# Four gate tiles move from single columns to column pairs of the seven-product form, and GpSimd takes part of the attention stage's vector work

## The chip, the cores and the metric

The kernel runs on one NeuronCore of a Trainium2 chip. A core has a matrix engine (TensorE, PE in the profile), a vector engine (VectorE, DVE), a scalar engine (ScalarE, ACT), GpSimd (POOL) and SyncE (SP), which issues the DMAs. The engines run their own instruction queues in order and meet at semaphores. The metric is the device time of one execution in microseconds (us); lower is better.

## The reference

One decoder block on a sequence of 1024 tokens of width 1024, all in float32. What matters here:

```
proj = rms_norm(x, ln1_g) @ w_in + b_in      # rq rk rv rg | aq ak av | gate_a gate_b
branch_a = (silu(rg) * head_group_norm(retention(rotary(rq), rotary(rk), rv))) @ w_ret_out
branch_b = sliding_window_sink_attention(rotary(aq), rotary(ak), av, sinks) @ w_attn_out
merged   = sigmoid(gate_a) * branch_a + sigmoid(gate_b) * branch_b
x = x + merged @ w_out
x = x + (silu(h2 @ w_ffn_gate) * (h2 @ w_ffn_up)) @ w_ffn_down    # h2 = rms_norm(x, ln2_g)
out = rms_norm(x, lnf_g)
```

`gate_a` and `gate_b` are 1024 columns each of the one projection: eight tiles of 128 columns each, called gate tiles 0 to 7 (first branch) and 8 to 15 (second). The attention has 16 query heads of 64, two key and value heads, blocks of 128 queries that look at 256 keys, and one sink per head.

## The kernel before

**Numbers.** A float32 operand is split into a high half in the fast matmul format (ScalarE, `copy`) and a low half, the rest (a subtraction), and a product is made of three matmuls: high by high, high by low, low by high. Every weight slab so costs one ScalarE cast and one subtraction (`split`, L129 to L137; for the query weights L401 and L402).

**Dense tiles.** `dense_g` makes one tile of 128 output columns for 1024 tokens: two halves of 512 tokens, 8 k-steps, 3 matmuls each, 48 matmuls of 128x512. Its weights (`slab`) pass through a ring of two buffers for high and low halves, so a new slab's halves are made when the tile two places earlier has done its last matmul.

**Column pairs.** After the attention the kernel computes wider pairs of tiles (256 columns, all 1024 tokens) with a seven-product scheme in the manner of Strassen: seven products of 12 matmuls, 84 in all, in place of 96. `cols` lists the pairs in order, `wseq` the order of their products, `wprep_to` makes the weight combinations (four GpSimd subtractions a pair, L555, and a split for each product, L130 and L133), `wproduct` multiplies, `wresult` evicts. Before, ten pairs are in `cols`: eight of the retention projections and two of the gates (tiles 2, 3 and 4, 5).

**The attention stage.** It has 32 units: four quads of four heads by eight blocks of queries. A unit u runs `u_scores` (eight matmuls of 256 columns into PSUM; for each of four heads a VectorE mask-and-minimum, L463, and a ScalarE exponential with its sum, L466; one reciprocal, L469; the four heads are scaled by it, L472 on ScalarE and L474 on VectorE, two each), `u_transpose` (eight transposes L484, then cast L487 and subtraction L488), and `u_values` (four matmuls L497 and L498, four small copies and sums L501 to L504, a split L506 and L507). GpSimd only puts the sink's column into the score tile `sc` (L451). Around the units stands fill, matmuls that wait for nothing of the units: `quad_q(g)` makes the queries of a quad (96 matmuls, then the rotation: eight VectorE and two ScalarE instructions a half, L419 to L428, into one buffer `stg`, and a round trip through DRAM), and `gate(n)` makes a dense gate tile, evicted with tanh (L513). `Fill` hands fill out in steps of three matmuls; the loop at the end of the stage gives each unit its share of `left` and lets `fl.until` force a quad's queries before its first unit. What stands on each engine's queue, and in which order, is chosen by the scheduler of the tile framework from the program order, priorities (`AHEAD`) and its own estimate; a queue then runs in exactly that order.

Fill before: queries of quads 1 to 3 and twelve gate tiles (6 to 15, 0, 1); of them the last three tiles are left for after the loop.

## Time and profile before

| what | value |
|---|---|
| time, median of 3 runs | 1584.97 us (1582.56 to 1584.98) |
| span of the profiled execution | 1583.3 us |
| PE, DVE, ACT, POOL busy, whole span | 1570.7, 990.2, 720.7, 354.9 us |
| loop over the attention units, first to last reciprocal | 101.9 to 323.6 us |
| seven-product stage of the pairs | about 435 to 626 us |
| granted TensorE clock | 0.999 |

The profiled execution's span is 1.7 us under the median of the runs. A row of a group of instructions reads: source line, engine, operation, output and inputs by the program's names, shapes, count | busy time, mean nanoseconds of one | idle time of the engine just before them and what ended it. A row of time reads: start, duration, engine, line, operation. Line numbers are those of the kernel before; the changed kernel's are one higher after the rotation's first new line.

### The profile page before, as it was taken

To read this page: it belongs to the slowest core of one execution; us is meant where nothing else is said; L and a number is where in the kernel's file an instruction comes from. 1 tells how busy PE (TensorE), PEld (TensorE's weight loads), DVE (VectorE), ACT (ScalarE), POOL (GpSimd) and SP (SyncE) were. 2 spreads that over 40 slices of the span, in tenths; PEclk is the share of its full clock that TensorE was granted. 3 is DMA by queue.
4 is the path that set the end of the run, shared out by engine and by line. 5 is a ranking of instruction groups with operands and counts; after the bars stand their busy time and mean duration, and the time that the engine had idled before them with its cause. 6 is when DMAs were issued, how large, how long until landed. Compare 5 with 4: busy or idle time off the path is not lost.

```text
span 1583.3 us, 20873 instructions
## 1 busy us (share of the span) xinstructions
PE 1570.7 (99%) x7483; PEld 1307.1 (83%) x7483; DVE 990.2 (63%) x1776; ACT 720.7 (46%) x1446; POOL 354.9 (22%) x303
## 2 busy tenths in 40 slices
PE   9999999999999999999999999999999999999998
PEld 8887888888888888888888888888888888888886
DVE  6469978777657663878544369444444444678656
ACT  5258877844233333544221256333333333344445
POOL 2000000000055441000000013555555555100001
PEclk9999999999999999999999999999999999999999
DMA  6564655440364455654545102333333333762333
GB/s 204 157 176 124 205 193 150 143 140 34 126 225 150 134 166 184 229 189 156 177 149 199 54 0 74 106 104 106 112 105 100 101 110 109 285 250 84 98 103 124
DMA packets 148886, 223.13 MB, mean 141 GB/s; under 512 B 9195, under 2 KB 81709, under 8 KB 147246
## 3 DMA queue, kind: packets, MB, share of 16 engines
q1 hardware_dynamic: 148780, 221.79, 43.3%
q8 instruction: 59, 0.97, 0.3%
q14 instruction: 45, 0.37, 0.1%
q10 hardware_dynamic: 2, 0.00, 0.0%
HBM read 149.67 MB, written 67.37 MB: 137 GB/s over the span
## 4 chain that ended last, share of the span: by engine, by line
PE 90%; ACT 6%; DVE 3%; issue 1%; POOL 0%; POOLq 0%; ACTq 0%; DVEq 0%
PE fA L1337 15%; PE fB L1337 8%; PE dA L1618 7%; PE wA L841 7%; PE dxP L1618 6%; PE fC L1337 4%; PE wB L841 3%; PE va L686 3%; ACT sc L466 2%; PE acc_g L157 2%; PE vP L686 2%; PE acc_g L158 2%; PE acc_g L159 2%; PE wo L1277 2%; PE wo L1276 2%; PE acc_ba L159 2%
## 5 line engine op out<-in xcount | busy, mean ns | idle before, releaser
L1618 PE MATMUL dA<-dwP,daP 128*128 128x512 f32 x528 | 120.6, 389 | 0.0
L1618 PEld LDWEIGHTS dA<-dwP,daP 128*128 128x128 f32 x528 | 99.0, 188 | 20.7 <-DVE dwP L133 0.2
L1618 PE MATMUL dxP<-dwP,daP 128*128 128x512 f32 x396 | 90.2, 389 | 0.0
L1618 PEld LDWEIGHTS dxP<-dwP,daP 128*128 128x128 f32 x396 | 74.3, 188 | 15.4
L157 PE MATMUL acc_g<-h,wh_g 128*128 128x512 f32 x192 | 75.5, 393 | 0.1
L158 PE MATMUL acc_g<-h,wh_g 128*128 128x512 f32 x192 | 75.2, 392 | 0.0
L159 PE MATMUL acc_g<-h,wl_g 128*128 128x512 f32 x192 | 75.1, 393 | 0.0
L466 ACT ACTIVATE sc<-sc,nm 128x257 f32<-128x257 f32 (+1 forms) x128 | 62.5, 492 | 27.1 <-DVE nm L463 26.7
L451 POOL COPY sc<-nsink 128x4 f32<-128x4 f32 x32 | 13.1, 412 | 274.4 <-PE pT L484 157.1
L1406 POOL TENSOR_TENSOR xf<-xf 128x512 f32<-128x512 f32 x40 | 61.2, 1531 | 30.4 <-issue 28.9
L1348 POOL TENSOR_TENSOR xf<-xf 128x512 f32<-128x512 f32 x33 | 49.4, 1496 | 54.3 <-ACT t_1P L130 22.4
L463 DVE CUSTOM_DVE_ANT_0 sc<-s,amask,nsink 128x256 f32<-128x256 f32 (+1 forms) x128 | 54.1, 461 | 9.8 <-PE s L460 9.5
L1358 ACT COPY xf<-fA 128x512 f32<-128x512 f32 x44 | 25.7, 586 | 74.4 <-PE fA L1337 74.4
L133 DVE TENSOR_TENSOR dwP<-wd,dwP 128x512 fp32r<-128x512 f32 x77 | 52.8, 685 | 6.0 <-ACT dwP L130 6.0
L130 ACT CAST dwP<-wd 128x512 fp32r<-128x512 f32 x77 | 47.4, 616 | 9.4 <-PE dA L1618 7.1
L157 PE MATMUL acc_bb<-ay,wh_bb 128*128 128x512 f32 x128 | 51.2, 400 | 0.0
L1523 POOL TENSOR_TENSOR rs_f<-tot,mhalf 128x1 f32<-128x1 f32 x8 | 4.8, 606 | 205.4 <-DVE tot L1520 205.4
L158 PE MATMUL acc_bb<-ay,wh_bb 128*128 128x512 f32 x128 | 50.3, 393 | 0.0
L159 PE MATMUL aq<-h,wl_aq 128*128 128x512 f32 x128 | 50.2, 392 | 0.0
L157 PE MATMUL aq<-h,wh_aq 128*128 128x512 f32 x128 | 50.1, 392 | 0.0
L158 PE MATMUL aq<-h,wh_aq 128*128 128x512 f32 x128 | 50.1, 391 | 0.0
L159 PE MATMUL acc_bb<-ay,wl_bb 128*128 128x512 f32 x128 | 50.1, 391 | 0.0
(794 smaller groups left out, 4356.9 us busy)
## 6 DMA issues: line engine op xcount, KB each, us to landing
act_d<-xf SPq DMA_DIRECT2D x77, 256.0 KB, 2.1
daP<-act_d SPq DMA_DIRECT2D x21, 512.0 KB
q_d<-stg SPq DMA_DIRECT2D x8, 1024.0 KB
q<-q_d SPq DMA_DIRECT2D x32, 256.0 KB, 6.5
ay_d<-q SPq DMA_DIRECT2D x8, 1024.0 KB
ay<-ay_d SPq DMA_DIRECT2D x4, 2048.0 KB, 14.2
wr_daP<-act_d SPq DMA_DIRECT2D x14, 512.0 KB, 3.7
wr_g<-in_w_in SPq DMA_DIRECT2D x12, 512.0 KB, 5.9
```

The source lines that it names most:

```text
L133: return nc.vector.tensor_tensor(out=lo, in0=raw, in1=f32(hi), op=ALU.subtract)
L157: nc.tensor.matmul(pt, hi[:, k, :], xh, start=(k == 0), stop=False)
L158: nc.tensor.matmul(pt, hi[:, k, :], xl, start=False, stop=False)
L159: nc.tensor.matmul(pt, lo[:, k, :], xh, start=False, stop=(k == 7))
L463: nc.vector.tensor_tensor_reduce(out=sc[:, j, 0:nk], in0=pt[:, jj * 256:jj * 256 + nk], in1=mk, scale=1.0, scalar=nsink[:, 4 * g + j:4 * g ...
L466: nc.scalar.activation(sc[:, j, 0:nk + 1], sc[:, j, 0:nk + 1], AF.Exp, scale=-1.0, bias=nm[:, j:j + 1], accum_out=den[:, j:j + 1])
L686: nc.tensor.matmul(vbanks[pr][tt], x_[:, c], w[:, u, :], start=(fresh and k + z == 0), stop=(k == 3 and z == 2), skip_group_check=not fresh)
L841: nc.tensor.matmul(pt, o[:, w, k, :], v, start=(first and k + z == 0), stop=(k == 3 and z == 2), skip_group_check=not first)
L1337: nc.tensor.matmul(pt, o[:, w, k, :], v, start=(first and k + z == 0), stop=(k == 3 and z == 2), skip_group_check=not first)
L1348: nc.gpsimd.tensor_tensor(out=dst[q], in0=dst[q], in1=sg[q], op=ALU.mult)
L1406: nc.gpsimd.tensor_tensor(out=o, in0=a, in1=b, op=op)
L1618: nc.tensor.matmul(banks[tt], a[:, u, c], w[:, v, :], start=(fresh and f + z == 0), stop=(f == NP - 1 and z == 2), skip_group_check=not fresh)
```

## The change

Tiles 0, 1, 6 and 7 leave the attention stage's fill and become two more column pairs in the seven-product stage, so that all eight gate tiles of the first branch are pairs (twelve pairs in `cols`). The fill keeps quads 1 to 3 and gate tiles 8 to 15, one gate behind each quad, the rest at the end; the count of steps follows, and three tiles are again left for after the loop. In the attention stage GpSimd makes the low halves of the gate weights and of the query weights of quads 1 to 3, three of the eight rotation steps of these quads (`s3 = b*cos`, `s0 = a*sin`, their sum), and the scaling of the fourth head of each unit, which ScalarE made.

```diff
-    def split(raw, hi, lo, hold=False):
+    def split(raw, hi, lo, hold=False, eng=None):
...
-            return nc.vector.tensor_tensor(out=lo, in0=raw, in1=f32(hi), op=ALU.subtract)
+            return (eng or nc.vector).tensor_tensor(out=lo, in0=raw, in1=f32(hi), op=ALU.subtract)
...
-                    nc.vector.tensor_tensor(out=lo, in0=rv_[:, :, z], in1=f32(hi), op=ALU.subtract)
+                    (nc.gpsimd if g else nc.vector).tensor_tensor(out=lo, in0=rv_[:, :, z], in1=f32(hi), op=ALU.subtract)
...
+                second = nc.gpsimd if g else nc.vector
+                second.tensor_tensor(out=s3, in0=b, in1=cos, op=ALU.mult)
+                nc.vector.tensor_tensor(out=s1, in0=b, in1=sin, op=ALU.mult)
                 nc.vector.tensor_tensor(out=s2, in0=a, in1=cos, op=ALU.mult)
-                nc.vector.tensor_tensor(out=s1, in0=b, in1=sin, op=ALU.mult)
+                second.tensor_tensor(out=s0, in0=a, in1=sin, op=ALU.mult)
                 nc.vector.tensor_tensor(out=s2, in0=s2, in1=s1, op=ALU.subtract)
-                nc.vector.tensor_tensor(out=s0, in0=a, in1=sin, op=ALU.mult)
-                nc.vector.tensor_tensor(out=s3, in0=b, in1=cos, op=ALU.mult)
-                nc.vector.tensor_tensor(out=s3, in0=s3, in1=s0, op=ALU.add)
+                second.tensor_tensor(out=s3, in0=s3, in1=s0, op=ALU.add)
...
-                if j % 2:
+                if j == 1:
                     nc.scalar.activation(sc[:, j, 0:nk], sc[:, j, 0:nk], AF.Copy, scale=rd[:, j:j + 1])
                 else:
-                    nc.vector.tensor_scalar(out=sc[:, j, 0:nk], in0=sc[:, j, 0:nk], scalar1=rd[:, j:j + 1],
-                                            scalar2=None, op0=ALU.mult)
+                    (nc.gpsimd if j == 3 else nc.vector).tensor_scalar(out=sc[:, j, 0:nk], in0=sc[:, j, 0:nk],
+                                                                       scalar1=rd[:, j:j + 1], scalar2=None, op0=ALU.mult)
...
-            return dense_g(w_in, C_GA + n * P, H, evac, f"g{n}")
+            return dense_g(w_in, C_GA + n * P, H, evac, f"g{n}", nc.gpsimd)
...
-        order = list(range(6, 16))
+        order = list(range(8, 16))
         gens = []
-        for g in range(4):
-            gens += [quad_q(g + 1)] if g < 3 else []
-            gens += [gate(n) for n in (order[2 * g:2 * g + 2] if g < 3 else order[6:] + [0, 1])]
+        for g in range(3):
+            gens += [quad_q(g + 1), gate(order[g])]
+        gens += [gate(n) for n in order[3:]]
...
-        left = 32 * 8 - 8 - 20
+        left = 32 * 3 + 16 * len(order) - 40 - 20
...
-                fl.until(3 * (i // NB - 1) + 1)
+                fl.until(2 * (i // NB - 1) + 1)
...
-    cols += [C_GA + 256, C_GA + 512]
+    cols += [C_GA + 256 * i for i in range(4)]
```

Three places of the order, before and after. In the names, `sc13` is the score tile of quad 1, block 3 (the number behind the underscore is the program's), `rd` its reciprocals, `wl` a low half, `g11` gate tile 11, `stg21` the rotation's buffer of quad 2, second half.

GpSimd's queue in the middle of quad 1's units, before:

```order
L451 COPY sc13_1825<-nsink_85 128x4
L451 COPY sc14_1908<-nsink_85 128x4
L451 COPY sc15_1992<-nsink_85 128x4
L451 COPY sc16_2081<-nsink_85 128x4
L451 COPY sc17_2164<-nsink_85 128x4
```

and in the change, from the same place and, behind the line of dots, the seven rows around gate 11's low half:

```order
L452 COPY sc14_1800<-nsink_85 128x4
L402 TENSOR_TENSOR wl_aq30_2087<-wr_aq30_2090,wh_aq30_2086 128x512
L475 TENSOR_SCALAR sc13_1727<-sc13_1727,rd13_1749 128x256
L420 TENSOR_TENSOR stg21_1833<-q211_1831,atab_176 128x512
L423 TENSOR_TENSOR stg21_1833<-q201_1539,atab_176 128x512
L452 COPY sc15_1899<-nsink_85 128x4
L425 TENSOR_TENSOR stg21_1833<-stg21_1833 128x512
...
L133 TENSOR_TENSOR wl_g10_2589<-wr_g10_2586,wh_g10_2588 128x1024
L452 COPY sc26_2626<-nsink_85 128x4
L133 TENSOR_TENSOR wl_g11_2875<-wr_g11_2872,wh_g11_2874 128x1024
L475 TENSOR_SCALAR sc25_2528<-sc25_2528,rd25_2550 128x256
```

Weight halves, rotation steps, scalings and sinks now stand in one queue; gate 11's low half stands ahead of unit 25's scaling.

VectorE's queue in the rotation of quad 2 (first half), before:

```order
L420 TENSOR_TENSOR stg20_1680<-q210_1678,atab_176 128x512
L423 TENSOR_TENSOR stg20_1680<-q210_1678,atab_176 128x512
L421 TENSOR_TENSOR stg20_1680<-stg20_1680 128x512
L424 TENSOR_TENSOR stg20_1680<-stg20_1680 128x512
L503 TENSOR_TENSOR tm10_1703<-pv10_1700,tm10_1703 64x256
L504 TENSOR_TENSOR tm10_1703<-pv10_1700,tm10_1703 64x256
L488 TENSOR_TENSOR pl110_1716<-pT110_1710,ph110_1715 128x512
L426 TENSOR_TENSOR stg20_1680<-stg20_1680 128x512
L428 TENSOR_TENSOR stg20_1680<-stg20_1680 128x512
```

and in the second half of quad 2 in the change:

```order
L421 TENSOR_TENSOR stg21_1833<-q211_1831,atab_176 128x512
L508 TENSOR_TENSOR q0_625<-tm12_1775,q0_625 128x2x128
L489 TENSOR_TENSOR pl130_1788<-pT130_1782,ph130_1787 128x512
L489 TENSOR_TENSOR pl131_1797<-pT131_1791,ph131_1796 128x512
L470 RECIPROCAL rd14_1822<-den14_1803 128x4
L422 TENSOR_TENSOR stg21_1833<-q201_1539,atab_176 128x512
L475 TENSOR_SCALAR sc14_1800<-sc14_1800,rd14_1822 128x256 x2
L424 TENSOR_TENSOR stg21_1833<-stg21_1833 128x512
```

The three steps that GpSimd has now (L420, L423, L425 there) are gone from it, and the units' own work stands between the rest.

PE's queue after the transposes of unit 33 (quad 3, block 3), before:

```order
L484 MATMUL pT330_3270<-ident_81,sc33_3198 128x128 x4
L484 MATMUL pT331_3279<-ident_81,sc33_3198 128x128 x4
L459 MATMUL s340_3292<-kst_180,q2_1416 128x256
...
L157 MATMUL acc_g13_0_3241<-h1_110,wh_g13_3237 128x512
L158 MATMUL acc_g13_0_3241<-h1_110,wh_g13_3237 128x512
L159 MATMUL acc_g13_0_3241<-h1_110,wl_g13_3238 128x512
...
L497 MATMUL pv33_3341<-ph330_3275,vst_181 128x512
```

and in the change:

```order
L485 MATMUL pT330_3056<-ident_81,sc33_3000 128x128 x4
L485 MATMUL pT331_3065<-ident_81,sc33_3000 128x128 x4
L159 MATMUL acc_g11_1_2963<-h1_110,wl_g11_2875 128x512
L498 MATMUL pv33_3127<-ph330_3061,vst_181 128x512
L499 MATMUL pv33_3127<-pl330_3062,vst_181 128x512
L498 MATMUL pv33_3127<-ph331_3070,vst_181 128x512
L499 MATMUL pv33_3127<-pl331_3071,vst_181 128x512
L460 MATMUL s340_3078<-kst_180,q2_1296 128x256
```

Where the eight scores of the next unit and 21 fill matmuls stood between transposes and value products, one fill matmul is left.

More of the change, by code (lines that the diff above doesn't have):

```diff
@@ L141, in release, with slab @@
             held.pop(0)()
-    def slab(src, col, name):
+    def slab(src, col, name, eng=None):
         with tc.high_priority(offset=AHEAD):
@@ L147, in slab @@
             hi, lo = hl_tiles([8, P], name)
-            split(raw, hi, lo)
+            split(raw, hi, lo, eng=eng)
         return hi, lo
@@ L174, in mm_halves, with dense_g @@
             nc.tensor.matmul(pt, wt[:, k, :], X[k // 4][:, 2 * (k % 4) + u, c0:c0 + n], start=(i == 0), stop=(i == 23))
-    def dense_g(src, col, X, evac, name):
-        w = slab(src, col, name)
+    def dense_g(src, col, X, evac, name, eng=None):
+        w = slab(src, col, name, eng)
         for half in range(2):
```

## The prediction

> **What bounds the kernel now.** I read the page's totals first, then busy time by stretch, then the groups of instructions of the attention stage, and last the order of time at single places.
>
> ```profile
> span 1583.3 us, 20873 instructions
> PE 1570.7 (99%) x7483; PEld 1307.1 (83%) x7483; DVE 990.2 (63%) x1776; ACT 720.7 (46%) x1446; POOL 354.9 (22%) x303
> ```
>
> PE is the bound of the whole, so matmuls are the currency. What one costs is read where nothing else happens. Busy time by stretch (span, then PE, PEld, DVE, ACT, POOL busy with counts, clock, DMA):
>
> ```profile
> 360.00:400.00 40.00, 40.00 (x178) 33.14 (x177) 31.84 (x40) 16.99 (x24) 0.00 (x0) 1.00 0.09 34
> 101.86:152.35 50.49, 49.94 (x273) 40.51 (x272) 48.19 (x147) 44.93 (x131) 2.69 (x8) 1.00 0.52 150
> 152.35:208.37 56.02, 55.44 (x291) 44.92 (x290) 49.61 (x148) 48.30 (x135) 4.15 (x8) 1.00 0.60 179
> 208.37:268.69 60.32, 59.03 (x316) 49.12 (x315) 52.52 (x150) 48.13 (x132) 4.11 (x8) 1.00 0.58 192
> 268.69:323.57 54.88, 54.23 (x290) 45.73 (x289) 36.92 (x115) 41.84 (x115) 1.85 (x6) 1.00 0.37 121
> 434.93:626.00 191.07, 190.88 (x841) 157.32 (x840) 112.57 (x132) 74.73 (x127) 81.84 (x56) 1.00 0.52 166
> L469 DVE RECIPROCAL rd<-den x32: 165/178/179, 101.9 to 323.6; 128x4 f32<-128x4 f32 x32
> ```
>
> The first row is a stretch of 512-wide matmuls alone: 40.00 / 178 = 0.2247 us each. The next four are the attention loop, cut at every eighth of the 32 reciprocals (one a unit); it lasts 221.7 us. There PE's busy time is no measure (ends are modelled), so I count its work:
>
> ```profile
> L159 PE MATMUL acc_g<-h,wl_g 128*128 128x512 f32 x130 | 51.0, 395 | 0.0
> L159 PE MATMUL aq<-h,wl_aq 128*128 128x512 f32 x64 | 25.3, 395 | 0.0
> L497 PE MATMUL pv<-ph,vst 128*128 128x512 f32 x56 | 22.7, 405 | 0.5 <-DVE tm L504 0.4
> L459 PE MATMUL s<-kst,q 128*128 128x256 f32 x108 | 28.8, 292 | 0.0
> L484 PE MATMUL pT<-ident,sc 128*128 128x128 f32 x232 | 33.7, 280 | 2.4 <-ACT sc L472 1.2 <-DVE sc L474 0.5 <-ACT tm L502 0.5
> 162.68 0.28 PE L459 MATMUL s<-kst,q 128*128 128x256 f32 x1
> 162.80 0.28 PE L460 MATMUL s<-kst,q 128*128 128x256 f32 x1
> 167.92 1.06 PE L484 MATMUL pT<-ident,sc 128*128 128x128 f32 x8
> ```
>
> With the sister lines, 3 x 130 + 3 x 64 + 2 x 56 = 694 matmuls of 512 take 155.9, 240 scores of 0.12 take 28.8 (the two start times), 232 transposes of about 0.11 take 25.5 (eight in 1.06, with 0.28 for the last): 210 us of work in 221.7, so PE wanders off for some 12 us. VectorE is busy 187.2 and ScalarE 183.2. In the first stretch VectorE is at 48.19 / 50.49 = 95%, and so is PE in the last (52 of 54.88 by count). So the loop runs at 95% of whichever engine is fullest, and the three are close.
>
> **The change part by part.** *Matmuls.* Four dense gate tiles leave the loop: 4 x 48 = 192 matmuls, 43.1 us. Two column pairs come into the seven-product stage: 2 x 7 x 12 = 168, 37.7 us. That stage is PE's own: in the 434.93:626.00 row VectorE has 112.57 of 191.07, GpSimd 81.84, so its added weight preparation hides and the 37.7 is paid in full. The loads stay 512 KB a tile. So the change gains only what the loop shrinks beyond 37.7; at best 5.4 for PE's work, plus stalls.
>
> *What leaves each engine in the loop.*
>
> ```profile
> L133 DVE TENSOR_TENSOR wl_g<-wr_g,wh_g 128x1024 fp32r<-128x1024 f32 x8 | 9.7, 1218 | 3.2 <-ACT wh_g L130 3.2
> L402 DVE TENSOR_TENSOR wl_aq<-wr_aq,wh_aq 128x512 fp32r<-128x512 f32 x8 | 5.4, 684 | 0.6 <-ACT wh_aq L401 0.5
> L507 DVE TENSOR_TENSOR q<-tm,q 128x256 fp32r<-128x256 f32 x30 | 12.5, 418 | 0.5 <-ACT q L506 0.3
> L130 ACT CAST wh_g<-wr_g 128x1024 fp32r<-128x1024 f32 x9 | 9.4, 1044 | 0.4 <-PE acc_g L158 0.3
> 167.12 0.91 ACT L472 ACTIVATE sc<-sc,rd 128x256 f32<-128x256 f32 x2
> ```
>
> VectorE loses all eight gate lows (9.7), eight query lows (8 x 0.60 from start to start = 4.8) and 3 of 8 rotation steps in six half quads (18 x 0.60 = 10.8): 25.3, leaving 161.9. ScalarE loses one scaling a unit (half of 0.91, x31 = 14.1) and four gates' casts and tanh (about 2.4 each, 9.6), leaving 159.5. PE is left with 210 - 43 = 167.
>
> *What GpSimd takes.* Unhindered, its 512-wide subtraction took 1.28:
>
> ```profile
> L361 POOL TENSOR_TENSOR wl_ak<-wr_kv,wh_ak 128x512 fp32r<-128x512 f32 x2 | 2.5, 1276 | 0.7 <-ACT wh_ak L356 0.7
> L451 POOL COPY sc<-nsink 128x4 f32<-128x4 f32 x2 | 0.3, 190 | 2.4 <-DVE nsink L298 2.4
> L555 POOL TENSOR_TENSOR wr_wp<-wr_wp 128x512 f32<-128x512 f32 x10 | 16.6, 1656 | 140.6 <-DVE w0P L133 122.5 <-DVE w9P L133 9.5 <-DVE w8P L133 2.4
> ```
>
> Rotation and query lows: 26 at 1.35, between the 1.28 and the 1.66 of the stage where VectorE works beside it: 35. Five gate lows of 1024 at 2.7 (2 x 1.28 to 2 x 1.66): 13.5. No row shows its scaling of 256: it lies between 0.19 (four elements copied) and 1.28 (512 from two sources); I take 0.6, half of the latter: 18.6 for 31. Sinks 5.9. Together 73 us, 38% of a loop of 190. That is no bound by itself. The question is what it does to VectorE, where both read their operands from SBUF:
>
> ```profile
> 450.38 1.74 POOL L812 TENSOR_TENSOR xw<-xw,rtabqT 128x512 f32<-128x512 f32 x1
> 450.89 1.78 DVE L813 TENSOR_TENSOR r<-r,rtabkT 128x512 f32<-128x512 f32 x1
> 452.60 0.68 DVE L133 TENSOR_TENSOR w0P<-wr_wp,w0P 128x512 fp32r<-128x512 f32 x1
> 169.20 2.23 POOL L451 COPY sc<-nsink 128x4 f32<-128x4 f32 x1 [9.05 <-PE pT L484]
> L821 DVE TENSOR_TENSOR r<-wB,u 128x512 f32<-128x512 f32 x11 | 7.6, 690 | 11.6 <-ACT u L846 8.4 <-PE wB L841 3.2
> 434.93:626.00 191.07, 69.17 (x68) 1.00 0.52 166
> 434.93:626.00 191.07, 13.09 (x16) 1.00 0.52 166
> 434.93:626.00 191.07, 13.42 (x16) 1.00 0.52 166
> ```
>
> VectorE's 0.68 product took 1.78 because GpSimd had begun 0.5 before; GpSimd's four-element copy took 2.23 instead of 0.19 during VectorE's rotation. Operations with one operand in PSUM (L821) keep their 0.69. The last three rows are VectorE's share of that stage for its lines with two SBUF operands (L133, L813, L816): 95.7 us for 100, against 68 unhindered: 0.28 lost per operation while GpSimd was busy 81.84 / 191.07 = 43%. At 38% that is 0.25. In the loop 30 rotation steps and 31 query lows (L507) remain on VectorE with two SBUF operands: 61 x 0.25 = 15 us of new waiting, which goes back onto VectorE: 162 + 15 = 177. So much of what it hands over returns as waits. The bounds of this term are 0 (GpSimd falls always between such operations) and 30 (twice, since the rotation runs on both at once by design). I take 15, the measured rate.
>
> The Trainium skill (Perfetto Trace Analysis, section Optimizing Scalar/DVE Operations) says of VectorE and GpSimd, which share a read port, that moving operations between the two "might not help". Taken to the full, all that is moved would come back as waits: 25.3 less the 4.9 of the four gates that vanish, 20.4 instead of 15, and about 1598 instead of the time below. The measured rate lies between that and free help, nearer to the rule.
>
> *By stretch*, since the loads are uneven. PE by count of the new order: 36.8, 41.3, 51.4, 35.9. VectorE: measured, less rotation (3.6 in each of the first three), query lows (2.4, 2.4), gate lows (1.2, 2.4, 2.4, 3.6), plus waits (4, 4, 4, 3): 45.0, 45.2, 50.5, 36.3. ScalarE, 3.6 less a stretch and a gate or two, is below these. The maxima add to 177.9; at 95%, 187.3.
>
> *Order.* After a unit's transposes PE needs fill until the probabilities are split: a ScalarE cast and a VectorE subtraction,
>
> ```profile
> L487 ACT CAST ph<-pT 128x512 fp32r<-128x512 f32 x58 | 31.6, 586 | 1.6 <-PE pT L484 1.2
> L488 DVE TENSOR_TENSOR pl<-pT,ph 128x512 fp32r<-128x512 f32 x58 | 39.1, 687 | 1.8 <-ACT ph L487 1.0
> ```
>
> so 0.59 to 1.27 us. In the order before, four units have under 0.9 us of PE work there; now 13 (one is shown above, a single fill matmul). Nine more at 0.4 (between 0, if the cast is prompt, and 0.9): 3.6 us. The loop: 190.9.
>
> *Sum.* The loop gives 221.7 - 190.9 = 30.8, the pairs take 37.7: plus 6.9. From the span of 1583.3 to 1590.2; on the median of the runs, 1584.97, it makes 1592.
>
> **The rivals.** *Faster: GpSimd is free help.* With no waits the maxima are 41.3, 42.3 (ScalarE), 51.4, 35.9 (PE): 170.9, at 95% 180, nothing bare: the loop gives 41.8 and the time is 1581. For it: VectorE's operations on PSUM, most of its loop, are not hindered. Against: L813.
>
> *No change.* Half the waits: maxima 173.6, loop 184.5, gain 37.2: 1585.5.
>
> *GpSimd's queue.* It runs in order, and a weight's low half that waits for its buffer stands ahead of a unit's scaling (the gate 11 row ahead of unit 25's in the order). Cast 1.04, low 2.7, scaling 0.6 make 4.3 from the release, and the transposes come after some 4.1 us of PE work: about 1.2 a place once ScalarE is late by one operation, at six such places 7 more: 1599. It decides if ScalarE's cast is not at once.
>
> *VectorE's scaling waits as well.* Its 256 elements from a single SBUF source,
>
> ```profile
> L474 DVE TENSOR_SCALAR sc<-sc,rd 128x256 f32<-128x256 f32 x54 | 16.7, 349 | 0.4
> L474 DVE TENSOR_SCALAR sc<-sc,rd 128x128 f32<-128x128 f32 x8 | 1.9, 282 | 0.1
> ```
>
> start at the same reciprocal as GpSimd's scaling. If they contend like the others, 62 x 0.25 = 15 more on VectorE; its sums are then the maxima, 192.7, the loop 206.4: 1607. No run here shows such a pair. The Trainium skill (SBUF — State Buffer, section Who interferes with whom) states that this operation, in its two-port mode, takes the shared ports too.
>
> **How the numbers follow.** Forecast 0.42, queue 0.10, scaling 0.07, no change 0.19, faster 0.22. A measurement here tells about 0.2% (3.2 us) from nothing. The forecast's own range is 1587 to 1597 by its terms (waits 10 to 20, bare places 0 to 8), a little of it (0.03) inside 0.2%: slower 0.56, same 0.22, faster 0.22. The range 1579 to 1603 leaves out the best of the faster case and the scaling rival.
>
> **What would show it.** The stretch of matmuls between loop and seven-product stage should keep 0.2247 each, and the latter should grow by 37.7. The loop, between first and last reciprocal, should be 191 long; VectorE still above 90% in it, with L421 and L508 well above 0.69 and 0.42 when GpSimd runs. If these keep their durations and the loop is under 183, the forecast is wrong. If VectorE has slack and PE waits for sc or wl from GpSimd, it is the queue.

## The result and the profile after

The changed kernel takes 1606.49 us (median of 4 runs, 1605.23 to 1608.21) beside 1584.23 for the kernel before on the same chip (4 runs, 1582.56 to 1584.98): a ratio of 1.0145, 95% interval 1.0130 to 1.0159. It is slower by 22 us; the forecast was 7 slower, 1592, with a range to 1603. The profiled executions differ by 20.5 (1603.8 beside 1583.3).

The page's totals of the changed kernel:

```profile
span 1603.8 us, 20935 instructions
PE 1576.9 (98%) x7459; PEld 1305.2 (81%) x7459; DVE 990.7 (62%) x1754; ACT 715.0 (45%) x1430; POOL 456.2 (28%) x381
```

VectorE has as much busy time as before (990.2), though it has less to do. Busy time by stretch (span, then PE, PEld, DVE, ACT, POOL busy with counts, granted clock, DMA share, GB/s): the whole attention loop between the first and the last reciprocal, its four parts of eight units, a stretch of matmuls alone, and the seven-product stage:

```profile
99.80:309.04 209.24, 192.55 (x983) 150.75 (x982) 182.98 (x522) 163.36 (x470) 85.64 (x90) 0.97 0.48 149
99.80:151.79 51.99, 46.62 (x244) 36.44 (x243) 47.17 (x134) 41.50 (x121) 26.71 (x27) 0.97 0.40 117
151.79:200.79 49.00, 46.13 (x246) 35.76 (x245) 47.05 (x138) 41.92 (x123) 21.59 (x24) 1.00 0.52 162
200.79:259.69 58.90, 53.87 (x272) 42.09 (x271) 52.40 (x146) 44.48 (x126) 22.41 (x23) 0.97 0.57 189
259.69:309.04 49.35, 45.94 (x226) 36.45 (x226) 36.36 (x111) 35.47 (x101) 14.94 (x16) 0.93 0.42 122
343.00:383.00 40.00, 40.00 (x178) 33.10 (x178) 31.84 (x40) 16.99 (x24) 0.00 (x0) 1.00 0.09 34
417.90:646.91 229.01, 228.83 (x1008) 188.70 (x1007) 125.49 (x152) 91.09 (x155) 91.95 (x64) 1.00 0.49 156
```

The matmul alone keeps its 40.00 / 178 = 0.2247. The pairs' stage grows from 191.1 to 229.0, by 37.9 (forecast 37.7). All of the miss is in the loop: it shrank from 221.7 to 209.2, by 12.5 where 30.8 was forecast. Places outside these two gave 4.9 together (the first reciprocal comes 2.1 earlier, the tail behind the loop is 2.6 shorter): 37.9 - 12.5 - 4.9 = 20.5.

In the loop VectorE is busy 183.0 (before 187.2) and ScalarE 163.4 (183.2). So neither is fuller than before and PE has 43 us less to do. Only in the second part is an engine at 95% or more (VectorE, 47.05 of 49.00); over the loop VectorE's 183.0 is 87%, where the prediction said above 90%. The last part is the farthest off: VectorE and ScalarE are busy 36.4 and 35.5 of 49.4, and PE ran at 0.93 of its clock.

Groups of instructions in that loop: one row of VectorE's rotation in the kernel before, then VectorE's and GpSimd's of the changed kernel (count | busy us, mean ns of one | idle time ahead of them):

```profile
L422 DVE TENSOR_TENSOR stg<-q,atab 128x512 f32<-128x512 f32 x6 | 4.1, 685 | 0.0
...
L475 DVE TENSOR_SCALAR sc<-sc,rd 128x256 f32<-128x256 f32 x54 | 26.0, 522 | 0.3
L508 DVE TENSOR_TENSOR q<-tm,q 128x256 fp32r<-128x256 f32 x30 | 14.6, 486 | 0.3
...
L422 DVE TENSOR_TENSOR stg<-q,atab 128x512 f32<-128x512 f32 x6 | 7.3, 1219 | 0.0
L421 DVE TENSOR_TENSOR stg<-q,atab 128x512 f32<-128x512 f32 x6 | 6.3, 1052 | 0.0
L424 DVE TENSOR_TENSOR stg<-stg 128x512 f32<-128x512 f32 x6 | 6.1, 1020 | 0.1
L427 DVE TENSOR_TENSOR stg<-stg 128x512 fp32r<-128x512 f32 x6 | 6.0, 1008 | 2.3 <-ACT stg L426 2.3
...
L475 POOL TENSOR_SCALAR sc<-sc,rd 128x256 f32<-128x256 f32 x27 | 27.2, 1009 | 56.6 <-DVE rd L470 56.6
L133 POOL TENSOR_TENSOR wl_g<-wr_g,wh_g 128x1024 fp32r<-128x1024 f32 x6 | 14.4, 2392 | 18.4 <-ACT wh_g L130 18.4
L425 POOL TENSOR_TENSOR stg<-stg 128x512 f32<-128x512 f32 x6 | 9.2, 1540 | 0.3
```

VectorE's scaling of 256 elements, 349 ns before, takes 522; the rotation steps, about 685 without GpSimd, take 1.0 to 1.2 us; the query low 486 beside 418. Summed: 54 x 0.173 + 30 x 0.068 + 6 x (0.534 + 0.367 + 0.335 + 0.323) = 9.3 + 2.0 + 9.4 = 20.7 us of standing still. What VectorE handed to GpSimd was, by the forecast's count, 20.4 (25.3 less the 4.9 of the four gates that left the loop). By the sum it came back whole; that the two agree so closely is in part chance, for in the other divisions below VectorE ends up to 3.7 under and 4.6 over the 182.8 that it has with nothing given away. GpSimd's own scaling takes 1.01, not the 0.6 that the forecast took.

One place where the waits join, in the order of time (start, duration, engine, line):

```profile
224.89 1.62 POOL L425 TENSOR_TENSOR stg<-stg 128x512 f32<-128x512 f32 x1
...
226.47 2.40 POOL L133 TENSOR_TENSOR wl_g<-wr_g,wh_g 128x1024 fp32r<-128x1024 f32 x1
...
226.55 0.63 ACT L426 ACTIVATE stg<-stg 128x512 fp32r<-128x512 f32 x1 [1.92 <-POOL stg L425]
...
227.21 2.21 DVE L427 TENSOR_TENSOR stg<-stg 128x512 fp32r<-128x512 f32 x1 [1.11 <-ACT stg L426]
...
227.61 1.05 ACT L488 CAST ph<-pT 128x512 fp32r<-128x512 f32 x2
...
229.35 0.68 DVE L429 TENSOR_TENSOR stg<-stg 128x512 fp32r<-128x512 f32 x1
...
230.06 0.43 DVE L505 TENSOR_TENSOR tm<-pv,tm 64x256 f32<-64x256 f32 x1
...
230.51 0.69 DVE L489 TENSOR_TENSOR pl<-pT,ph 128x512 fp32r<-128x512 f32 x1
...
230.63 0.47 PE L498 MATMUL pv<-ph,vst 128*128 128x512 f32 x1 [1.20 <-DVE tm L505]
...
231.26 0.50 PE L499 MATMUL pv<-pl,vst 128*128 128x512 f32 x1 [0.16 <-DVE pl L489]
```

ScalarE stands 1.92 behind GpSimd's last rotation step, whose input buffer it is to overwrite. GpSimd goes on with a gate's low half at 226.47. VectorE's remainder (0.69 alone) starts beside it and takes 2.21: it ends 0.55 after GpSimd's low half, at 229.42. Behind it in VectorE's queue stand L505, the last sum over the values of the unit before, and L489, the low half of this unit's probabilities, whose cast had begun at 227.61. PE's first product of values waits 1.20 for L505, and the second 0.16 for L489.

A second place, in the last part of the loop, where no rotation is left:

```profile
284.77 2.38 POOL L133 TENSOR_TENSOR wl_g<-wr_g,wh_g 128x1024 fp32r<-128x1024 f32 x1 [7.08 <-ACT wh_g L130]
...
285.44 2.35 DVE L475 TENSOR_SCALAR sc<-sc,rd 128x256 f32<-128x256 f32 x2
...
287.13 1.92 POOL L475 TENSOR_SCALAR sc<-sc,rd 128x256 f32<-128x256 f32 x2
```

GpSimd had stood idle for 7.08 until the gate's cast was done, and then began the gate's low half just before a unit's reciprocal (285.22 to 285.40). VectorE's two scalings of that unit (0.35 each before) take 2.35 beside it, and GpSimd's own starts 1.7 late. This is what the prediction's queue rival described, a low half ahead of a unit's scaling, with the port's price on top.

### The profile page after: what moved, and what is told of

It reads as the page before. It is cut to its first block, busy times and chain, and to the rows that moved or that the text cites. A ratio compares the mean times of both kernels' runs of the same rounds, so it can differ in the third digit from the quotient of the medians.

```text
span 1603.8 us, 20935 instructions
## 1 busy us (share of the span) xinstructions
PE 1576.9 (98%) x7459; PEld 1305.2 (81%) x7459; DVE 990.7 (62%) x1754; ACT 715.0 (45%) x1430; POOL 456.2 (28%) x381
## 4 chain that ended last, share of the span: by engine, by line
PE 90%; DVE 3%; ACT 3%; issue 2%; POOL 1%; DMA 0%; POOLq 0%; ACTq 0%; DVEq 0%
PE fA L1338 15%; PE wA L842 8%; PE fB L1338 7%; PE dA L1619 7%; PE dxP L1619 6%; PE wB L842 4%; PE fC L1338 4%; PE va L687 3%; PE vP L687 2%; PE wC L842 2%; PE wo L1277 2%; PE wo L1276 2%; PE acc_ba L158 2%; PE acc_ba L159 2%; PE wo L1278 2%; PE acc_ba L157 2%
## 5 line engine op out<-in xcount | busy, mean ns | idle before, releaser
L1619 PEld LDWEIGHTS dA<-dwP,daP 128*128 128x128 f32 x528 | 99.0, 188 | 20.7 <-DVE dwP L133 0.2
L1619 PEld LDWEIGHTS dxP<-dwP,daP 128*128 128x128 f32 x396 | 74.3, 188 | 15.4
L1349 POOL TENSOR_TENSOR xf<-xf 128x512 f32<-128x512 f32 x33 | 49.4, 1496 | 54.5 <-ACT t_1P L130 22.4
L556 POOL TENSOR_TENSOR wr_wp<-wr_wp 128x512 f32<-128x512 f32 x12 | 19.5, 1622 | 129.7 <-issue 92.6
L556 POOL TENSOR_TENSOR wr_f<-wr_f 128x512 f32<-128x512 f32 x20 | 30.3, 1514 | 78.7 <-DVE t_4P L133 8.7
L1007 POOL TENSOR_TENSOR grs<-gve,mhalf 128x2 f32<-128x2 f32 x16 | 11.3, 705 | 145.2 <-DVE gve L1005 145.2
L157 PE MATMUL acc_g<-h,wh_g 128*128 128x512 f32 x128 | 52.0, 406 | 0.4 <-ACT wh_g L130 0.4
L159 PE MATMUL acc_g<-h,wl_g 128*128 128x512 f32 x128 | 51.3, 402 | 0.9 <-POOL wl_g L133 0.9
L475 POOL TENSOR_SCALAR sc<-sc,rd 128x256 f32<-128x256 f32 (+1 forms) x32 | 31.2, 975 | 72.6 <-DVE rd L470 72.6
L158 PE MATMUL acc_g<-h,wh_g 128*128 128x512 f32 x128 | 51.7, 404 | 0.0
L157 PE MATMUL aq<-h,wh_aq 128*128 128x512 f32 x128 | 51.1, 399 | 0.0
```

The source lines that it names most:

```text
L157: nc.tensor.matmul(pt, hi[:, k, :], xh, start=(k == 0), stop=False)
L158: nc.tensor.matmul(pt, hi[:, k, :], xl, start=False, stop=False)
L159: nc.tensor.matmul(pt, lo[:, k, :], xh, start=False, stop=(k == 7))
L556: nc.gpsimd.tensor_tensor(out=o, in0=a, in1=b, op=ALU.subtract)
L1619: nc.tensor.matmul(banks[tt], a[:, u, c], w[:, v, :], start=(fresh and f + z == 0), stop=(f == NP - 1 and z == 2), skip_group_check=not fresh)
```

## The experiments

Each ratio is against the kernel before, measured on the same chip together with the run (medians 1582.9 to 1584.9). Differences between two rows are taken from the times as they stand; with these medians up to 1.9 apart and intervals of about 2.4 to each side, a difference of 1 to 3 us is not told from nothing. "Loop" is first to last reciprocal; VectorE and GpSimd are their busy time in it.

| kernel | time us | ratio, 95% | loop | VectorE | GpSimd |
|---|---|---|---|---|---|
| before | 1584.23 | | 221.7 | 187.2 | 12.8 |
| changed | 1606.49 | 1.0145 (1.0130 to 1.0159) | 209.2 | 183.0 | 85.6 |
| e4: tiles alone | 1595.11 | 1.0069 (1.0054 to 1.0084) | 198.9 | 182.8 | 12.4 |
| e19: tiles, lows | 1592.18 | 1.0048 (1.0031 to 1.0065) | 196.5 | 182.1 | 33.1 |
| e17: tiles, rotation | 1596.42 | 1.0080 (1.0065 to 1.0095) | 199.2 | 182.1 | 31.0 |
| e2: tiles, lows, scaling | 1593.07 | 1.0055 (1.0040 to 1.0070) | 199.2 | 186.3 | 64.1 |
| e3: tiles, rotation, scaling | 1599.85 | 1.0100 (1.0083 to 1.0117) | 201.6 | 187.4 | 61.4 |
| e1: tiles, lows, rotation | 1603.91 | 1.0119 (1.0104 to 1.0134) | 206.7 | 179.1 | 51.6 |
| e5: all three, tiles as before | 1603.33 | 1.0122 (1.0105 to 1.0139) | 240.4 | 186.6 | 92.5 |
| e8: lows, scaling, tiles as before | 1587.89 | 1.0031 (1.0020 to 1.0041) | 226.6 | 186.1 | 70.0 |
| e16: three pairs, nothing on GpSimd | 1587.68 | 1.0030 (1.0018 to 1.0041) | 208.9 | 184.9 | 11.3 |

### One part undone at a time

e1 gives the fourth head's scaling back to ScalarE:

```diff
-                if j == 1:
+                if j % 2:
```

> The change with one part undone: the fourth head's scaling is back on ScalarE, all else as changed. The changed kernel took 1606.5 us, its loop from first to last reciprocal 209.2. Ports (VectorE's two remaining scalings wait for GpSimd's, 0.18 us each on average by the trace of the change, and GpSimd holds some 30 us less): loop 200 or less, time 1594 to 1599, VectorE's scaling back at 0.35 us. Thin fill (the order on PE leaves too little between a unit's steps, whoever scales): loop 207 to 210, time 1604 to 1607. ScalarE's load as the bound: loop longer, 1612 or more, since ScalarE gets 14 us back.

Measured: 1603.91, 2.6 better than the changed kernel; ScalarE 174.8 in the loop, VectorE 179.1. That is close to the time of "thin fill". VectorE's scaling does not go back to 0.35 but to 0.46, beside GpSimd's lows and rotation.

e2 gives the rotation back to VectorE:

```diff
-                second = nc.gpsimd if g else nc.vector
+                second = nc.vector
```

> The change with the rotation of quads 1 to 3 back on VectorE alone. Ports: 10.8 us of work come back to VectorE, and the waits of its rotation steps (13 us over the plain duration in the change) go; the two cancel within 3 us, time 1603 to 1609. GpSimd's queue as the cause (scalings stand behind rotation steps of 1.4 us): GpSimd's scalings start sooner, time 1598 to 1601. Thin fill: 19 units instead of 13 have under 0.9 us of PE work behind their transposes in the order, so slower, 1609 to 1612.

Measured: 1593.07, 13.4 better, the largest of the three and below all three expectations.

e3 gives the low halves back to VectorE:

```diff
-                    (nc.gpsimd if g else nc.vector).tensor_tensor(out=lo, in0=rv_[:, :, z], in1=f32(hi), op=ALU.subtract)
+                    nc.vector.tensor_tensor(out=lo, in0=rv_[:, :, z], in1=f32(hi), op=ALU.subtract)
...
-            return dense_g(w_in, C_GA + n * P, H, evac, f"g{n}", nc.gpsimd)
+            return dense_g(w_in, C_GA + n * P, H, evac, f"g{n}")
```

> The change with the weights' low halves back on VectorE. Ports: VectorE gets 10 us of work back and loses a few us of waits, so 1606 to 1612. Late weights (a low half takes GpSimd 2.4 us behind other work, the next gate tile's fill is not ready, and the order leaves PE without fill in the last seven units): the last quarter of the loop shrinks from 49 us to 40 and the time falls to 1596 to 1600.

Measured: 1599.85, 6.6 better. This is the second expectation, late weights, in both of its numbers: the last part of the loop takes 41.2 where the changed kernel's took 49.4.

```profile
262.23:303.46 41.23, 41.04 (x223) 33.52 (x222) 35.84 (x111) 35.35 (x101) 8.49 (x13) 1.00 0.41 128
```

PE does nearly the same there, 223 matmuls against 226. The 8 us are lost wherever lows and rotation are both on GpSimd and the order leaves that much to the last part: 49.8 in e1 (228 matmuls) and 49.4 in e6 (226), but 41.8 in e17 (223) and 40.3 in e4 (217).

e4 undoes all three, with the diffs of e1, e2 and e3 together; only the tiles are moved:

> The moved tiles alone: nothing goes to GpSimd. Ports: no VectorE operation of the loop is over its plain duration; VectorE's load is 182 us as before less four gate lows, so the loop is 190 to 196 and the time 1591 to 1597, less than with the help of GpSimd. GpSimd's help as a real relief that was too small: the loop is longer than 209 and the time over 1607.

Measured: 1595.11. The loop of e4:

```profile
99.76:298.62 198.86, 188.51 (x985) 149.96 (x984) 182.81 (x552) 174.14 (x502) 12.44 (x30) 0.97 0.50 158
```

So the tiles alone cost 10: their pairs are paid with 38, the loop gives 22.8 and the rest of the kernel some 5. GpSimd's help, meant to let the loop follow PE, costs 11.4 more. What the three are worth does not add: 2.6 + 13.4 + 6.6 is twice 11.4.

### One part alone, and GpSimd's help without the tiles

e17 is e4 with the rotation on GpSimd, e19 is e4 with the lows there (the diffs above, the other way):

> All tiles moved, and of the three kinds of work only half of q's rotation on GpSimd; scalings and lows stay where they were. Beside the kernel with nothing on GpSimd (1595.1, loop 198.9) and that with scalings and lows there (1593.1). If the rotation is dear by itself, through ports and waits at its own place: 1602 to 1607, as in the changed kernel. If it is dear because GpSimd's queue then holds the fourth head's scalings and the lows back: nothing else stands in the queue here, 1593 to 1598.

> All tiles moved, the weights' and queries' lows on GpSimd, rotation and scalings as before the change. VectorE gives up 4 gate lows and 8 query lows, 9 to 10 us; the port price for 20 us of GpSimd's time is, by the dummies (8.3 for 26), 6.5. If relief and price add: 1592 to 1595 beside 1595.1. If lows in GpSimd's queue are dear by themselves (their users on PE wait): 1597 or more.

Measured: rotation alone 1596.42, 1.3 above e4. VectorE has 17 instructions fewer in the loop, about 11 us at 0.68 each, but only 0.7 less busy time (182.1 as against 182.8). Lows alone 1592.18, 2.9 below e4, the fastest of the seven divisions with the tiles moved. Both came out as the milder expectation said, and neither differs from e4 by more than the runs can tell. So the rotation is not dear by its place alone. It costs 13.4 in company (e2 to changed), 1.3 by itself. e1, read beside these, says which company: lows and rotation together, with no scaling on GpSimd, are already 8.8 above e4 (1603.91), and their loop is 7.8 longer.

e5 and e8 leave the tiles as before. e5 has all three kinds on GpSimd; e8 is e5 with the rotation on VectorE:

```diff
-        order = list(range(8, 16))
+        order = list(range(6, 16))
...
-    cols += [C_GA + 256 * i for i in range(4)]
+    cols += [C_GA + 256, C_GA + 512]
```

> The tiles stay divided as before (ten gate tiles and two column pairs as in the kernel before); only the three kinds of work go to GpSimd. Ports (what leaves VectorE comes back as waits): VectorE stays busy 183 to 188 in the loop, GpSimd about 95, and PE has its 210 of work and so more to fill with than the changed kernel; the loop is 222 to 228, the time 1585 to 1592. GpSimd's chain (rotation steps of 1.3 to 1.5 us, ScalarE held behind them): what the offload cost on top of the tiles, 11.4, is paid here too whatever PE has to fill with: loop 233, time 1596. Free help (the offload is good where PE has work enough): VectorE 165, loop 216, time 1579.

> The tiles stay divided as before, the fourth head's scaling and the weights' and queries' lows go to GpSimd, the rotation stays on VectorE. If the rotation is what makes GpSimd's help cost: the two others are worth what they were worth with all tiles moved (1595.1 to 1593.1, so 2 us), loop 219.5, time 1583. If the port takes back what is given (VectorE still busy 185): no change, 1585 within 3. If PE's work of 210 is the bound here, any relief of VectorE and ScalarE brings the loop towards 214 at most: 1577.

Measured: e5 1603.33, worse than any of the three expectations; e8 1587.89. GpSimd's help costs 20.4 where PE still has its 210 us of work, more than the 11.4 with the tiles moved. So it is no matter of too little work for PE; VectorE is at 186.6 and 186.1, next to 187.2 with nothing given away. Here too the rotation in company is the dear part: e5 lies 15.4 above e8, which came out as the expectation said in which VectorE gets back what it gave.

### What a GpSimd operation does to VectorE

e9 runs operations alone and then side by side, 12 or 16 of VectorE's against 6 or 8 of GpSimd's (the five kinds, with their lines):

```diff
+ nc.vector.tensor_scalar(out=o[:, 0:256], in0=go[:, 0, 0:256], scalar1=rcol[:, 0:1], scalar2=None, op0=ALU.mult)   # L65
+ nc.vector.tensor_tensor(out=o[:, 0:256], in0=go[:, 0, 0:256], in1=go[:, 1, 0:256], op=ALU.add)                    # L67
+ nc.vector.tensor_tensor(out=o, in0=pt, in1=go[:, 1, :], op=ALU.subtract)                                          # L69, pt in PSUM
+ nc.gpsimd.tensor_scalar(out=o[:, 0:256], in0=go[:, 0, 0:256], scalar1=rcol[:, 0:1], scalar2=None, op0=ALU.mult)   # L75
+ nc.gpsimd.tensor_tensor(out=o, in0=go[:, 0, :], in1=go[:, 1, :], op=ALU.mult)                                     # L77
```

> Computes nothing of the reference: a row of sections of VectorE and GpSimd operations, each alone and then both at once. VectorE: a scaling of 256 from one SBUF source, an addition of 256 from two SBUF sources, a subtraction of 512 with one operand in PSUM; GpSimd: a scaling of 256, a product of 512 from two sources. Ports by two-source operations only: VectorE's scaling alone 0.35 and beside GpSimd 0.35; addition alone 0.42 and beside GpSimd's product 0.6 or more; PSUM subtraction 0.69 both times. Ports for its single-source scaling too: scaling beside GpSimd's product 0.5 or more, up to the 1.3 of a whole product, and beside GpSimd's scaling as well. GpSimd alone: scaling 0.6 (forecast) to 1.0 (as in the loop), product 1.28.

Its order of time, rows of one kind drawn together (start, time for all of them, engine, line, count):

```profile
15.21 3.24 DVE L65 TENSOR_SCALAR da<-go,rcol 128x256 f32<-128x256 f32 x12 [15.21 <-DMA rcol<-in_c_rcol]
...
19.14 4.11 DVE L67 TENSOR_TENSOR da<-go 128x256 f32<-128x256 f32 x12 [0.69 <-ACT go L83]
...
24.53 7.26 DVE L69 TENSOR_TENSOR da<-pt,go 128x512 f32<-128x512 f32 x12 [1.28 <-ACT go L83]
25.11 7.24 POOL L75 TENSOR_SCALAR pa<-go,rcol 128x256 f32<-128x256 f32 x8 [24.69 <-ACT go L83]
...
34.34 7.36 POOL L77 TENSOR_TENSOR pa<-go 128x512 f32<-128x512 f32 x6 [1.99 <-ACT go L83]
...
42.40 10.33 DVE L65 TENSOR_SCALAR da<-go,rcol 128x256 f32<-128x256 f32 x16 [10.60 <-ACT go L83]
43.02 7.71 POOL L77 TENSOR_TENSOR pa<-go 128x512 f32<-128x512 f32 x6 [1.32 <-ACT go L83]
...
53.42 11.84 DVE L67 TENSOR_TENSOR da<-go 128x256 f32<-128x256 f32 x16 [0.70 <-ACT go L83]
53.53 8.44 POOL L77 TENSOR_TENSOR pa<-go 128x512 f32<-128x512 f32 x6 [2.79 <-ACT go L83]
...
66.56 7.26 DVE L69 TENSOR_TENSOR da<-pt,go 128x512 f32<-128x512 f32 x12 [1.30 <-ACT go L83]
66.67 7.39 POOL L77 TENSOR_TENSOR pa<-go 128x512 f32<-128x512 f32 x6 [4.70 <-ACT go L83]
...
74.75 7.34 DVE L65 TENSOR_SCALAR da<-go,rcol 128x256 f32<-128x256 f32 x16 [0.93 <-ACT go L83]
74.81 7.58 POOL L75 TENSOR_SCALAR pa<-go,rcol 128x256 f32<-128x256 f32 x8 [0.76 <-ACT go L83]
```

Alone a VectorE scaling takes 3.24 / 12 = 0.27. Sixteen would be 4.32, and beside GpSimd's products they take 10.33: 6.0 lost while GpSimd worked 7.71. Sixteen additions lose 11.84 - 5.48 = 6.4 of 8.44. The subtraction with an operand in PSUM takes 7.26 both times and loses nothing. So VectorE stands still for three quarters of a GpSimd product, whether its own operation has one SBUF source or two, and GpSimd loses 0.0 to 1.1 beside its 7.36 alone. Beside GpSimd's scalings it loses less: 7.34 - 4.32 = 3.0 of 7.58, 40%. GpSimd's scaling takes 7.24 / 8 = 0.91 alone. So the second expectation holds, that the single-source scaling waits for the port too. The Trainium skill (SBUF — State Buffer, section Who interferes with whom) says that the shared port pair is an exclusive lock which a scaling takes too in its two-port mode, and that an operation with at most one SBUF input outside that mode is free of it; 10.33 for 4.32 and 7.26 for 7.26 agree.

e18 puts work on GpSimd that nobody waits for into the kernel with only the tiles moved: three operations of 128x512 at each of the six half quads, in a scratch tile of their own.

```diff
+                if g:
+                    dum = gt.tile([P, 512], F32, tag="dum", bufs=1, name=f"dum{g}{half}")
+                    nc.gpsimd.tensor_tensor(out=dum, in0=b, in1=cos, op=ALU.mult)
+                    nc.gpsimd.tensor_tensor(out=dum, in0=sin, in1=cos, op=ALU.mult)
+                    nc.gpsimd.tensor_tensor(out=dum, in0=cos, in1=sin, op=ALU.add)
...
-                t = gt.tile([P, 512], F32, tag="st", bufs=2, name=f"tb{n}{half}")
+                t = gt.tile([P, 512], F32, tag="st", bufs=1, name=f"tb{n}{half}")
```

> All tiles moved, nothing of the three kinds of work on GpSimd, but three 128x512 operations for each of the six half quads there, into a scratch tile of their own that nobody reads (and one buffer instead of two for the tanh of the gates). GpSimd's queue holds otherwise only the sinks' copies. If the ports make GpSimd's rotation dear: VectorE's rotation steps (0.68 us) take 0.9 or more, its scaling 0.35 stays or rises to 0.4, loop 204 or more, time 1600 to 1606. If ports cost only where something waits for GpSimd: 1594 to 1597, as without the dummies (1595.1).

Measured: 1603.38, ratio 1.0126 (1.0109 to 1.0143), 8.3 above e4. Its loop:

```profile
100.10:306.43 206.33, 189.59 (x982) 148.58 (x981) 190.30 (x552) 173.92 (x501) 31.36 (x45) 0.97 0.48 151
```

VectorE is 7.5 fuller than in e4 and the loop 7.5 longer; five of the eight rotation steps take 0.81 to 1.05 us, the scaling keeps 353 ns. The first expectation holds. This is the port price nearly by itself (a tanh waited once, 1.0, for its one buffer): what VectorE stood still, the loop became longer.

e10 and e15 put the same dummies into e2, beside lows and scaling. In e10 they shared the buffers of the gates' tanh, in e15 they have their own (and the tanh one buffer, as in e18).

> The changed kernel with q's whole rotation on VectorE; GpSimd does, at the places of its three rotation steps, three products and sums of the same 128x512 size into a scratch tile that nobody reads. Between 1593.1 (rotation on VectorE, GpSimd free of it) and 1606.5 (the changed kernel). If ports alone make the rotation on GpSimd dear: the 26 us of dummies take from VectorE, whose operations with SBUF operands stand still for three quarters of a GpSimd operation, at least 8 us; loop 207 or more, time 1601 to 1607. If the waits do it (ScalarE held in order behind GpSimd's last step, VectorE's remainder behind ScalarE): nobody waits for the dummies, loop 199 to 202, time 1593 to 1596.

> The dummies again, in a scratch tile of their own, now beside the scalings and lows on GpSimd and with q's rotation on VectorE (1593.1 without dummies). Nothing on VectorE, ScalarE or PE waits for a dummy, but dummies stand in GpSimd's queue ahead of scalings and lows, and they hold the port. If the port alone counts: the same 8 as in the kernel with nothing else on GpSimd, 1601. If the full queue of GpSimd is what makes the rotation there cost 13 in company and 1 alone: 1605 to 1610, as in the changed kernel or above.

Measured: e10 1610.44, ratio 1.0163 (1.0147 to 1.0180), but it is not clean; a tanh waited for a dummy's buffer:

```profile
ACT tb L519 <- POOL dum L430: 6.0, 1, 6.0
```

e15 1604.04, ratio 1.0131 (1.0116 to 1.0146): 11.0 above e2, between the 8 of the port alone and the 12 that would have spoken for the queue. VectorE 192.4, 6.0 over e2, loop 206.5, 7.3 longer. In time that is most of the rotation's 13.4 in company, but the way there is another. In e15 VectorE becomes fuller and the loop follows it: 93% in e15, 94% in e2 (186.3 of 199.2). In the changed kernel VectorE has 3.3 less to do than in e2 and the loop is 10.0 longer, 87%. So dummies at the rotation's places do not stand for the rotation in company. (They also delay a query's low half on GpSimd, for which PE waits once, 2.9.)

### Scaling left out, and VectorE's sum

e6 leaves out the fourth head's scaling in the changed kernel (`range(4)` becomes `range(3)`):

> The changed kernel with the fourth head's scaling left out altogether (its probabilities stay undivided, so the output is another); PE's order is the changed kernel's. If GpSimd's scaling hinders VectorE's (L475, 522 ns instead of 349) and the transposes wait for it: VectorE's scaling falls back below 420 ns, the loop shortens by 9 or more from 209 to 200 or less, time 1597 or less. If the rotation and the lows set the pace: the loop keeps 204 to 209 and the time is 1601 to 1606, no better than with that scaling on ScalarE (1603.9).

Measured: 1600.18, ratio 1.0103 (1.0088 to 1.0118), loop 204.9. It lies between the two theories, nearer to the second. VectorE's scaling falls to 457 ns, not below 420: rotation and lows still stop it.

e14 leaves out VectorE's two scalings a unit in e4:

```diff
-            for j in range(4):
+            for j in range(1, 4, 2):
```

> Only the tiles moved (all pairs, nothing on GpSimd: 1595.1, loop 198.9, VectorE busy 182.8, PE's work 167), and VectorE's two scalings a unit left out altogether: heads 0 and 2 stay undivided, so the output is another. This is relief of VectorE by 18.6 us that nobody has to pay. If VectorE's sum sets this loop at 92%: loop 198.9 - 18.6 / 0.92 = 179, time 1575, well under the kernel before. If latency along a unit's chain and ScalarE (174) set it: loop 190 to 195, time 1586 to 1591.

Measured: 1588.44, ratio 1.0031 (1.0020 to 1.0042). Its loop:

```profile
100.05:291.18 191.13, 183.49 (x984) 146.18 (x983) 167.59 (x490) 173.70 (x502) 10.63 (x30) 0.98 0.52 163
```

VectorE has 15.2 less to do than in e4, free of any price, and the loop is 7.7 shorter. That is the second theory's range: VectorE's sum alone does not set this loop. The theory names two things, waits along a unit's chain and ScalarE, and e14 does not part them: ScalarE is now the fullest engine, 173.7 of 191.1, which is 91%, as VectorE was at 92% in e4.

e16 makes three pairs instead of two or four (ten gate tiles in the loop, nothing on GpSimd):

```diff
-        order = list(range(8, 16))
+        order = list(range(8, 16)) + [0, 1]
...
-    cols += [C_GA + 256 * i for i in range(4)]
+    cols += [C_GA + 256 * i for i in range(1, 4)]
```

> Nothing on GpSimd; three column pairs instead of the two of the kernel before and the four of the changed one, so ten gate tiles in the loop instead of twelve and eight. A pair costs 18.9. If each pair of tiles taken from the loop gives the same (22.8 for two pairs, so 11.4 each): 1590, loop 210. If the loop is PE's while PE has the most work and only the second pair is lost: the first gives 2 x 10.8 = 21.6, loop 200, time 1582, better than both kernels. If latency holds the loop already: it gives 8 or less, time 1596.

Measured: 1587.68. The loop gives 12.8 for the first pair's two tiles and 10.0 for the second's, where PE's work falls by 21.6 each time and a pair costs 19. Both pairs lose, nearly alike, as the first expectation said.

### The late roundings

e11 issues the roundings of the rotated queries after the next unit's scores, and rounds the first half into the buffer that VectorE alone has read:

```diff
-                nc.scalar.activation(s0.bitcast(F32R), s2, AF.Copy)
-                nc.vector.tensor_tensor(out=s2.bitcast(F32R), in0=s2, in1=s0, op=ALU.subtract)
...
+                def rest(s=(s0, s1, s2, s3), stg=stg, g=g, half=half, Bt=Bt, jb=jb, c=c):
+                    nc.scalar.activation(s1.bitcast(F32R), s2, AF.Copy)
+                    nc.vector.tensor_tensor(out=s2.bitcast(F32R), in0=s2, in1=s1, op=ALU.subtract)
...
+                late.append(rest)
...
                 u_scores(i)
+                flush()
```

> The changed kernel; q's rotation stays half on GpSimd, but ScalarE's two roundings of the rotated q and VectorE's two remainders are issued after the next unit's scores, and the first rounding goes to the buffer that only VectorE has read, so it no longer waits for GpSimd. If the waits behind GpSimd's last step cost the 13.4: most comes back, ScalarE's wait on the roundings (9.1 us) falls below 3, the loop to 196 to 202, time 1593 to 1598. If the ports do it: they are as before, loop 206 to 210, time 1603 to 1607.

> The kernel before with the same late roundings and nothing on GpSimd: a control for what the lateness itself does. No wait for GpSimd is there to be taken away, so both theories say the same: the loop 219 to 224, time 1582 to 1588. If it comes out more than 3 away, the run with late roundings in the changed kernel is not to be read as the wait alone.

Measured: e11 1602.34, ratio 1.0117 (1.0102 to 1.0132), 4.1 better than the changed kernel; e13, the control, 1587.39, ratio 1.0024 (1.0015 to 1.0034), 4.3 worse than the kernel before, and so by its own expectation (more than 3 away) e11 is not to be read as the wait alone. Nor was the wait taken away: the framework's scheduler put the second rounding ahead of the first in ScalarE's queue, where GpSimd's last step was not done.

```profile
ACT stg L437 <- POOL stg L432: 11.5, 5, 4.1
```

So e11 settles nothing on what ScalarE's waits behind GpSimd cost. No version was faster than the kernel before.

## Why the prediction was wrong

**Right.** The pairs' 37.7 (37.9 measured), the pitch of 0.2247, that PE's work leaves the loop without the loop following, that much of what VectorE hands over returns as waits, the sign. The loop's rows for L421 and L508 rose as said.

**The waits, 15 forecast, 20.7 measured.** The term was made of 61 operations with two SBUF operands, and VectorE's scaling was left out of it as a rival at 0.07. That rival's mechanism is real: its 54 scalings lost 9.3, and e9 shows it by itself. The other 11.4 are near the 15. The rival's loop, 206.4, and its 1607 came close to what happened, but partly by luck: its sum of 30 us of waits did not come true, since VectorE ended at 183.0 and not 192.7, and the loop was long for another reason. GpSimd's scaling was a second mis-sized price (0.6 taken, 1.01 measured): 11.6 of the 13 by which GpSimd's time, 86, is over the 73 forecast. The sentence on the Trainium skill (Perfetto Trace Analysis, section Optimizing Scalar/DVE Operations), that work moved between the two "might not help", was the better guide: in seven ways of dividing the three kinds with the tiles moved, VectorE's busy time stays between 179.1 and 187.4, whatever is handed over.

**The step that failed: "the loop runs at 95% of whichever engine is fullest".** With VectorE at its true 183.0 the rule still gives 183.0 / 0.95 + 3.6 = 196.2, 5.3 over the forecast's 190.9; the loop took 209.2, 13.0 more. The 95% was read from a loop in which PE had 210 us of work to fill with. The share of the fullest engine in the runs (PE, by its work of 210 or 189, in the kernel before, e8, e5 and e16) is:

| runs | share |
|---|---|
| before | 95% |
| tiles moved, lows and rotation not both on GpSimd (e2, e3, e4, e17, e19) | 91 to 94% |
| e16, e8 | 90%, 93% |
| lows and rotation both on GpSimd (changed, e1, e5, e6 with VectorE at 178.7 of 204.9, e11 at 182.0 of 208.1) | 87% |

At the 92% of e4 a VectorE of 183.0 makes 198.9. So some 3 of the 13.0 come with PE's smaller work, and some 10 with lows and rotation standing on GpSimd together, with or without the scaling and with the tiles moved or not. Apart, neither has that price. What these 10 consist of is argued, not shown: by the two places above they are waits between the engines, behind GpSimd's queue and the port, 8 of them in the last part of the loop. The queue rival, at 0.10, had such a place; it priced six of them at 7. The term for bare places (3.6) was meant to hold PE's waits and was too small, and it counted the wrong thing: e2 has more of them in its order (19) than the changed kernel (13), and a loop shorter by 10.

**The clock, not in the forecast at all.** In the changed kernel's loop four windows of 3.4 us run at half clock (below); in the loop before there is none. An estimate of what they cost, from the matmuls that start in them: 23 of 512 columns, 0.43 from start to start where nothing else delays them and 0.2247 elsewhere, and 12 of 256 columns, 0.21 and 0.12: 23 x 0.20 + 12 x 0.09 = 5.7 us of PE's time. How much of it made the loop longer is not shown: e4 has three such windows and is at 92%, e19 has none and is at 93%.

So the 18.3 by which the loop was missed are 5.3 of VectorE's waits and 13.0 of the rule, in which the clock has at most some 6; what was saved outside the loop, 4.9, was not forecast either.

**What stays open.** Lows alone change e4 by -2.9, rotation alone by 1.3, both by 8.8, all three by 11.4. Why the first two cost together what neither costs apart is not shown. The scheduler may order every queue anew in each of these runs, and none of them holds the order fixed. The places at 226 and 285 us are examples of how the waits join, not a measure of their sum.

## What to carry to other kernels

Work given from VectorE to GpSimd is priced by what VectorE runs at the same time. By e9, count every VectorE operation whose operands are all in SBUF, scalings with one source too, as standing still for three quarters of each GpSimd operation with two sources beside it (40% beside a GpSimd scaling), and only those with an operand in PSUM as free. A share like "95% of the fullest engine" belongs to the loop it was read in: before work is taken from the engine that fills the gaps, try that removal alone: here 43 us less for PE returned 22.8. Two kinds of work that are each cheap on an engine can be dear together on it, so try them singly and in pairs. Where PE's gaps grow, look at the granted clock in windows of 3.4 us, for a gap can be paid twice.
